# Weight loads ordered behind the newest transposes of queries and keys, and output stores behind the newest transpose of probabilities, in a two-layer attention trunk

## The chip, the cores and the metric

The kernel runs on one core of a Trainium2 chip. The metric is the device time of one execution in microseconds (us). TensorE (PE) multiplies matrices, VectorE (DVE), ScalarE (ACT) and GpSimd (POOL) work on tiles element by element, and SyncE (SP) issues every DMA of this kernel, all on one queue.

## The reference

Two layers on a sequence of 1024 tokens with width 1024. Layer 0 mixes tokens by dilated sliding-window attention (mixer A, three groups, merged by their softmax denominators), layer 1 by grouped-query attention with a window of 128 and learned sinks (mixer B). Shortened:

```python
def reference(x, p, ...):
    for i in range(DEPTH):                      # DEPTH = 2
        h = mixer_a(...) if i % 3 == 0 else mixer_b(...)
        x = layer_norm(ALPHA * x + h, ln_g[i], ln_b[i])
        gate = sigmoid(x @ ple_w_gate[i])
        x = x + gate * (p[i] @ ple_w_proj[i])

def mixer_a(x, w_in, w_out, cos, sin):
    h = x @ w_in
    for gi, (window, dil) in enumerate(A_GROUPS):    # (128,1), (512,4), (2048,16)
        q, k, v = ...                                # 16 heads of 64, q and k rotated
        o, lse = banded_attention(strided(q), strided(k), strided(v), window // dil)
    o = sum over groups of softmax(lse) * o
    return (o * silu(z)) @ w_out
```

`banded_attention` takes softmax(q k / 8) over a causal band and multiplies by v.

## The kernel before

**Linear products.** Each weight matrix is cut into blocks of 512 columns (33 blocks, numbered here in the order of their use; layer A has blocks 0 to 19 of its input matrix, then 20 and 21 of its output matrix). `Block.load` (line 97) brings a block in four DMAs of 512 KB (`wraw`, line 102). `maxima` (line 108, DVE) finds its largest value, `split` (lines 131 and 132, ACT and DVE) writes it as two float16 parts. `weight_steps` strings this together: block i+2 is loaded as soon as block i has been split, since there are two buffers for `wraw`. `lin` (lines 270 to 272) makes one 128x512 tile of a product from 24 matmuls, in about 5.2 us.

**Attention.** In layer A a run of three blocks is values, queries and keys, queries and keys. After each tile of queries and keys `rope_out` rotates it on DVE and POOL (lines 345 to 359) and transposes it by a DMA, `qk<-hl` (line 360; `bq` and `bk` in layer B). A "unit" is 128 queries of four heads. `scores` multiplies queries and keys (line 383), takes the mask and the row maximum on DVE (line 387), the exponentials on ACT (line 393), splits the probabilities into two float16 parts (lines 397 and 399) and transposes them by a DMA, `pT<-phl` (line 402, the P transpose). `pv` multiplies the transposed probabilities by the values (lines 414 to 416). `outp` evicts the result to `st` and stores it to DRAM, `scr<-st` (line 703). There are 96 units in layer A and 32 in layer B, numbered here from 0 in the order in which they are scored. A unit's `pv` is issued two units after its scores in layer A, three in layer B, so that softmax and transpose have time meanwhile. Layer A's outputs are read back (`gt<-scr`, line 745), merged over the three groups (`merge`) and stored (`oa<-gt`, line 767). In layer B the stores are `ob<-mu` (line 860), and the gate's rows are `za<-zu` and `zb<-zu` (line 725).

**What sets the order.** The kernel is written as one stream of operations; a scheduler, which works with estimated durations, puts each engine's instructions into an order. On the chip an engine takes its own in that order and waits where one's inputs are not there. SP too is such an engine: a DMA whose buffer is not free holds up all DMAs behind it.

Of the kernel before, what the change touches and what calls it, by code (L numbers as in the profile page):

```python
# [2 lines left out]

# [1 line left out]

# [83 lines left out]
class Block:  # L89
# [5 lines left out]

    def load(self):
        k = self.k
        self.n = NK * self.cols
        self.raw = k.raw.tile([P, NK * 512], F32, tag="wraw", name="wraw")
        q = self.n // 4  # L100
        for c in range(4):
            k.nc.sync.dma_start(self.raw[:, c * q:(c + 1) * q], self.src[:, c * q:(c + 1) * q])
# [36 lines left out]
class Trunk:  # L139
    def __init__(self, ctx, tc, a):  # L140
        self.ctx, self.tc, self.nc, self.a = ctx, tc, tc.nc, a
        nc = self.nc
        ec = ctx.enter_context
        self.const = ec(tc.tile_pool(name="const", bufs=1))
        self.small = ec(tc.tile_pool(name="small", bufs=2))
        self.raw = ec(tc.tile_pool(name="raw", bufs=2))
        self.wp = ec(tc.tile_pool(name="wp", bufs=2))
        self.ps_lin = ec(tc.tile_pool(name="ps_lin", bufs=3, space=PSUM))
        self.ps_s = ec(tc.tile_pool(name="ps_s", bufs=4, space=PSUM))
        self.ps_o = ec(tc.tile_pool(name="ps_o", bufs=1, space=PSUM))  # L150
        self.dram = ec(tc.tile_pool(name="dram", bufs=1, space=DRAM))
        self.o_ps = self.ps_o.tile([P, 2, 4, HD], F32, tag="o", name="o")
        self.o_i = 0
        self.uid = 0
        self.bufs = 2
        self.pw = self.wg = None
        self.due = []
        self.merges, self.merging = [], []
        self.merge_wait, self.merge_every = 0, 1
        self.units = []  # L160
        self.upt = 1.0
        self.pipe = [None, None]
        self.credit = 0.0
        self.ends = []
        self.work_done = 0.0
        self.tile_w = 1.0
        self.step_credit = 0.0

        tab = self.const.tile([P, N_CONST], F32, name="tab")
        self.tab = tab  # L170
        b = 0
        self.mask_a = tab[:, b:b + 2 * P]
        self.mask_b = tab[:, b + 2 * P:b + 4 * P]
        self.mask_2 = tab[:, b + 4 * P:b + 5 * P]
        self.ident = tab[:, b + 5 * P:b + 6 * P]
        self.ones = self.const.tile([P, P], BF16, name="ones")
        nc.gpsimd.memset(self.ones, 1.0)
        self.ones32 = self.const.tile([P, 1], F32, name="ones32")
        nc.gpsimd.memset(self.ones32, 1.0)
        self.mhalf = self.const.tile([P, 1], F32, name="mhalf")  # L180
        nc.gpsimd.memset(self.mhalf, -0.5)
        self.sinks = self.const.tile([P, 16], F32, name="sinks")
# [152 lines left out]
    def rope_out(self, ps, nq, nk, n, dst):  # L335

        nc, w = self.nc, self.work
        nh = nq + nk  # L340
        t1 = w.tile([P, 512], F32, tag="t1", name="t1")
        t2 = w.tile([P, 512], F32, tag="t2", name="t2")
        pv = ps.rearrange("p (h c) -> p h c", c=32)
        cos = self.cos[:, n, :].unsqueeze(1).to_broadcast([P, 2 * nh, 32])
        nc.vector.tensor_mul(t1[:, :nh * HD].rearrange("p (h c) -> p h c", c=32), pv, cos)  # L345
        pb = ps.rearrange("p (h b c) -> p h b c", b=2, c=32)[:, :, ::-1, :]
        sin = self.sin[:, n].unsqueeze(1).to_broadcast([P, nh, 2, 32])
        nc.vector.tensor_mul(t2[:, :nh * HD].rearrange("p (h b c) -> p h b c", b=2, c=32), pb, sin)  # L348
        nc.gpsimd.tensor_add(t1[:, :nh * HD], t1[:, :nh * HD], t2[:, :nh * HD])  # L349
        nb = nh + nk  # L350
        hl = w.tile([P, 12, P], F16, tag="hl", name="hl", bufs=3)
        rv = t1[:, :nh * HD].rearrange("p (h c) -> p h c", c=HD)

        def parts():
            nc.scalar.activation(hl[:, :nh, 0:HD], rv, AF.Copy)  # L355
            nc.gpsimd.tensor_sub(hl[:, :nh, HD:P], rv, hl[:, :nh, 0:HD])  # L356
            if nk:
                src, to = (hl[:, a:b, :].rearrange("p h (w c) -> p h w c", w=2) for a, b in ((nq, nh), (nh, nb)))
                nc.vector.tensor_copy(to, src[:, :, ::-1, :])  # L359
            nc.sync.dma_start(dst, hl[:, :nb, :].rearrange("p b c -> p (b c)"), transpose=True)  # L360

        self.ends.append(parts)

# [6 lines left out]
    def scores(self, qa, kas, mask, cs, ncs, sums, nbias, floor, pool_lo):  # L370
# [28 lines left out]
        eng.tensor_sub(hl[:, 1], sm[:, :, :nk], hl[:, 0])  # L399
        pt = at.tile([P, 2, 4, 2, P], F16, tag="pT", name="pT", bufs=len(self.pipe) + 1)  # L400
        ptf = pt.rearrange("p a h b c -> p (a h b) c")[:, :8 * nb, :]
        nc.sync.dma_start(ptf, pf[:, :8 * nk], transpose=True)
        return ptf.rearrange("p (a h b) c -> p a h b c", a=2, h=4)

    def pv(self, pt, va, vla):
# [278 lines left out]
    def unit_a(self, q, g, n, qk, vh, vl, cs, ncs, cv, scr):  # L684
        nc, at = self.nc, self.att
        tiles = [n] if g == 2 or (n % 2 == 0 if g == 1 else n == 0) else [n - 1, n]
        mask = self.mask_2 if g == 2 else self.mask_a[:, (2 - len(tiles)) * P:]

        def stats():
            st = at.tile([P, 4 * HD + 8], F32, tag="st", name="st", bufs=len(self.pipe) + 2)  # L690
            return st, st[:, 4 * HD:4 * HD + 4], st[:, 4 * HD + 4:]

        def outp(o, st):
            nc.scalar.activation(st[:, 0:4 * HD], o.rearrange("p h c -> p (h c)"), AF.Copy, scale=cv)
            d = scr[q // 2][g][:, q % 2, :]
            if g == 1:
                b = 512 * (n % 2) + n // 2
                d = d[b:b + 509:4]
            elif g == 2:
                d = d[n:n + 1017:8]  # L700
            else:
                d = d[n * P:(n + 1) * P]
            nc.sync.dma_start(d, st)
            if g == 0 and q % 2:
                self.merges.append(self.merge(n, q // 2, scr[q // 2]))

        kas = [lambda h, sw, t=qk[i]: t[:, 4 + 4 * sw + h, :] for i in tiles]
        self.later(UNIT_LAG, lambda: self.unit(lambda h: qk[n][:, h, :], kas, mask, cs, ncs,
                                          lambda h, kb: vh[:, tiles[kb], h, :], lambda h, kb: vl[:, tiles[kb], h, :],
                                          stats, outp, n % 4 != 0))  # L710
# [16 lines left out]
    def z_block(self, invx, stat):  # L727

        self.z_stat = stat
        self.upt = 2.0  # L730
        for half in range(2):
            self.w_z = self.next_block()
            self.cz = self.prod(invx, self.w_z.inv, 0.5, "cz")
            for n in range(Z_AHEAD if half else NT):
                self.z_tile(self.work, n, half)
                self.progress()
            if half == 0:
                self.w_z.released = True
# [405 lines left out]
```

## Time and profile before

| what | value |
|---|---|
| median of 3 runs | 1685.56 us (1683.73 to 1686.35) |
| the profiled execution | 1685.33 us |
| its span, first to last instruction | 1683.5 us |
| PE busy | 1595.0 us, 95% of the span |
| mean granted TensorE clock | 0.984 |

The table says that PE works nearly all the time, so a microsecond is won or lost where PE stands idle or runs at its lower clock. A PE that is "busy" is not at its peak: matmuls overlap in the record. What counts is the interval from one start to the next.

### The profile page before, as it was taken

The page shows a single profiled execution, that of the slowest core. Times are in us where ns is not written, and L with a number is a line of the kernel's source. Part 1 is how long each engine was busy: PE and PEld are TensorE (multiplying, and loading weights), DVE is VectorE, ACT ScalarE, POOL GpSimd, SP SyncE. Part 2 cuts the span into 40 slices and gives each one's busy share as a digit, 9 for nine tenths or more (in the row PEclk, how much of TensorE's full clock was granted, in tenths as well). Part 3 has the DMA queues.
Part 4 walks back from the last instruction along what each step waited for, and adds up shares of the span by engine and source line. Part 5 has one row for each costly group of instructions (what it writes and reads, how often), then busy time and mean ns, then how long its engine had stood idle before and what let it go on. Part 6 is the DMA issues. An engine that isn't in the chain of part 4 may idle for free. (4 is left out here: it accounts for less than half of the span.)

```text
span 1683.5 us, 29019 instructions
## 1 busy us (share of the span) xinstructions
PE 1595.0 (95%) x10579; PEld 881.5 (52%) x10579; DVE 1130.6 (67%) x2721; ACT 871.7 (52%) x1946; POOL 677.5 (40%) x481
## 2 busy tenths in 40 slices
PE   9898999999999889999999988898999998999999
PEld 3455566654555445766545544344455555544444
DVE  6767556665667776566656696887447898778631
ACT  4525564564755355655647662633232888853321
POOL 0215423532554565234325654443323552225441
PEclk9999999999999999999999999899999999999999
DMA  9617855773678668557647986989965798987963
GB/s 361 242 60 160 171 145 123 174 159 108 140 160 219 190 137 176 151 132 163 155 114 157 193 224 208 316 242 276 233 179 133 139 207 176 182 292 219 248 209 113
DMA packets 543791, 311.02 MB, mean 185 GB/s; under 512 B 473120, under 2 KB 494240, under 8 KB 543392
## 3 DMA queue, kind: packets, MB, share of 16 engines
q1 hardware_dynamic: 543648, 309.16, 74.1%
q8 instruction: 83, 1.36, 0.3%
q14 instruction: 60, 0.49, 0.1%
HBM read 137.78 MB, written 54.92 MB: 114 GB/s over the span
## 5 line engine op out<-in xcount | busy, mean ns | idle before, releaser
L270 PE MATMUL lin<-whl,xhl 128*128 128x512 f16 x1280 | 491.2, 384 | 0.0
L271 PE MATMUL lin<-whl,xhl 128*128 128x512 f16 x1280 | 490.3, 383 | 0.0
L272 PE MATMUL lin<-whl,xhl 128*128 128x512 f16 x1280 | 489.9, 383 | 0.0
L349 POOL TENSOR_TENSOR t<-t,t 128x512 f32<-128x512 f32 (+1 forms) x120 | 152.4, 1270 | 265.2 <-DVE t L348 233.0
L399 POOL TENSOR_TENSOR phl<-sm,phl 128x1024 f16<-128x1024 f32 (+1 forms) x88 | 156.9, 1783 | 245.4 <-ACT phl L397 217.8
L108 DVE TENSOR_REDUCE wpm<-wraw 128x1 f32<-128x1024 f32 (+1 forms) x132 | 157.1, 1198 | 92.6 <-DMA wraw<-in_wa_dram 48.2
L272 PEld LDWEIGHTS <-xhl 128*128 128x128 f16 x1280 | 149.5, 117 | 128.0 <-issue 5.3
L270 PEld LDWEIGHTS <-xhl 128*128 128x128 f16 x1280 | 149.5, 117 | 120.1 <-issue 5.4
L271 PEld LDWEIGHTS <-xhl 128*128 128x128 f16 x1280 | 150.4, 117 | 118.1 <-issue 5.3
L393 ACT ACTIVATE sm<-sm,st,cs 128x128 f32<-128x128 f32 (+1 forms) x384 | 203.6, 532 | 3.8 <-ACT mw L752 0.3
L356 POOL TENSOR_TENSOR hl<-t,hl 128x512 f16<-128x512 f32 (+1 forms) x120 | 145.4, 1212 | 124.6 <-ACT hl L355 124.6
L387 DVE CUSTOM_DVE_ANT_0 sm<-s,tab 128x256 f32<-128x256 f32 (+1 forms) x512 | 156.9, 359 | 33.6 <-PE s L383 31.9
L355 ACT ACTIVATE hl<-t 128x512 f16<-128x512 f32 (+1 forms) x120 | 72.3, 603 | 190.6 <-POOL t L349 181.5
L132 DVE SCALAR_TENSOR_TENSOR whl<-wraw,s,whl 128x1024 f16<-128x1024 f32 (+1 forms) x116 | 161.4, 1445 | 3.1 <-ACT whl L131 3.0
L131 ACT ACTIVATE whl<-wraw,s 128x1024 f16<-128x1024 f32 (+1 forms) x116 | 121.9, 1123 | 26.6 <-PE lin L272 10.2
L270 PE MATMUL lin<-whl,x2T 128*128 128x512 f16 (+1 forms) x320 | 115.5, 361 | 0.0
L271 PE MATMUL lin<-whl,x2T 128*128 128x512 f16 (+1 forms) x320 | 115.2, 360 | 0.0
L272 PE MATMUL lin<-whl,x2T 128*128 128x512 f16 (+1 forms) x320 | 115.2, 360 | 0.0
L397 ACT ACTIVATE phl<-sm 128x1024 f16<-128x1024 f32 (+1 forms) x128 | 110.7, 865 | 3.6 <-DMA pT<-phl 1.6
L345 DVE TENSOR_TENSOR t<-lin,rope 128x512 f32<-128x512 f32 (+1 forms) x120 | 78.9, 658 | 47.2 <-PE lin L272 46.9
L359 DVE COPY hl<-hl 128x512 f16<-128x512 f16 (+1 forms) x104 | 55.7, 535 | 74.7 <-POOL hl L356 74.6
L414 PEld LDWEIGHTS <-pT 128*128 128x128 f16 x800 | 72.8, 99 | 46.4 <-DMA pT<-phl 44.0
(190 smaller groups left out, 2913.7 us busy)
## 6 DMA issues: line engine op xcount, KB each, us to landing
wraw<-in_wa_dram SPq DMA_DIRECT2D x56, 512.0 KB, 5.1
scr<-st SPq DMA_DIRECT2D x96, 132.0 KB, 2.4
gt<-scr SPq DMA_DIRECT2D x48, 264.0 KB, 3.5
wraw<-in_wav_dram SPq DMA_DIRECT2D x24, 512.0 KB, 5.6
prh<-pro SPq DMA_DIRECT2D x32, 256.0 KB, 4.4
wraw<-in_wg_dram SPq DMA_DIRECT2D x16, 512.0 KB, 7.7
wraw<-in_wb_dram SPq DMA_DIRECT2D x16, 512.0 KB, 6.7
xg<-y SPq DMA_DIRECT2D x16, 512.0 KB, 3.8
```

What stands on the lines that cost most here:

```text
L108: k.nc.vector.tensor_reduce(pm[:, c:c + 1], self.raw[:, c * q:(c + 1) * q], axis=AX.X, op=ALU.max, apply_absolute_value=True)
L131: nc.scalar.activation(hl[:, 0, sl], self.raw[:, sl], AF.Copy, scale=self.s)
L132: nc.vector.scalar_tensor_tensor(hl[:, 1, sl], self.raw[:, sl], self.s, hl[:, 0, sl], op0=ALU.mult, op1=ALU.subtract)
L270: mm(ps, xh(kt), wh, start=(kt == 0), stop=False)
L271: mm(ps, xh(kt), wl, start=False, stop=False)
L272: mm(ps, xl(kt), wh, start=False, stop=(kt == NK - 1))
L349: nc.gpsimd.tensor_add(t1[:, :nh * HD], t1[:, :nh * HD], t2[:, :nh * HD])
L356: nc.gpsimd.tensor_sub(hl[:, :nh, HD:P], rv, hl[:, :nh, 0:HD])
L387: nc.vector.tensor_tensor_reduce(sm[:, h, :nk], ps[:, i, :nk], mask, 1.0, -3e38, ALU.add, ALU.max, mx[:, h:h + 1])
L393: nc.scalar.activation(sm[:, h, :nk], sm[:, h, :nk], AF.Exp, bias=nbias[:, h:h + 1], scale=cs, accum_out=sums[:, h:h + 1])
L397: nc.scalar.activation(hl[:, 0], sm[:, :, :nk], AF.Copy)
L399: eng.tensor_sub(hl[:, 1], sm[:, :, :nk], hl[:, 0])
```

## The change

Two ties are added, both by `issue_after(ins)`, which lays an ordering edge (no wait on a semaphore) from an instruction to those that the block issues on the same engine, here SP. First, the four DMAs of a weight load stand behind the transpose of queries and keys that was written last (`self.moved`) when `load` is called; `z_block` clears this mark, so that loads called from there on are free until layer B's first transpose. Second, the store of a unit in layer A stands behind the P transpose that was written last (`self.p_moved`), which is that of a unit scored later. Nothing is computed differently, and no instruction is added or removed on any engine.

```diff
     def load(self):
+        k = self.k
+        with k.tc.issue_after(k.moved.ins) if k.moved else nullcontext():
+            self.transfers()
+
+    def transfers(self):
         k = self.k
         self.n = NK * self.cols
         self.raw = k.raw.tile([P, NK * 512], F32, tag="wraw", name="wraw")
...
         self.o_i = 0
         self.uid = 0
+        self.moved = self.p_moved = None
...
-            nc.sync.dma_start(dst, hl[:, :nb, :].rearrange("p b c -> p (b c)"), transpose=True)
+            self.moved = nc.sync.dma_start(dst, hl[:, :nb, :].rearrange("p b c -> p (b c)"), transpose=True)
...
-        nc.sync.dma_start(ptf, pf[:, :8 * nk], transpose=True)
+        self.p_moved = nc.sync.dma_start(ptf, pf[:, :8 * nk], transpose=True)
...
-            nc.sync.dma_start(d, st)
+            with self.tc.issue_after(self.p_moved.ins):
+                nc.sync.dma_start(d, st)
...
     def z_block(self, invx, stat):
 
         self.z_stat = stat
+        self.moved = None
         self.upt = 2.0
```

Since the scheduler starts anew from these edges, the order changes in other places too. (The changed file has eight more lines, so line 402 is line 408 there, 360 is 366, 102 is 107, 703 is 710, 414 is 420, 270 to 272 are 276 to 278 and 383 is 389.)

SP's queue at the load of block 11 (`wraw_5139`), while layer A's tiles 39 to 44 of queries and keys are made (`qk_` and `pT_` with their numbers are the transposes; `scr0` is a store). Before:

```order
L703 DMA scr0_0_617<-st_4511 128x264
L102 DMA wraw_5139<-in_wa_dram 128x1024
L360 DMA_TRANSPOSE qk_4724<-hl_4730 128x12x128
L402 DMA_TRANSPOSE pT_4764<-phl_4761 128x16x128
L703 DMA scr0_0_617<-st_4613 128x264
L360 DMA_TRANSPOSE qk_4828<-hl_4834 128x12x128
L102 DMA wraw_5139<-in_wa_dram 128x1024 x3
L402 DMA_TRANSPOSE pT_4885<-phl_4882 128x16x128
```

Now:

```order
L366 DMA_TRANSPOSE qk_4724<-hl_4730 128x12x128
L408 DMA_TRANSPOSE pT_4764<-phl_4761 128x16x128
L710 DMA scr0_0_617<-st_4511 128x264
L366 DMA_TRANSPOSE qk_4828<-hl_4834 128x12x128
L408 DMA_TRANSPOSE pT_4885<-phl_4882 128x16x128
L710 DMA scr0_0_617<-st_4613 128x264
...
L366 DMA_TRANSPOSE qk_5067<-hl_5073 128x12x128
L107 DMA wraw_5139<-in_wa_dram 128x1024 x4
L408 DMA_TRANSPOSE pT_5107<-phl_5104 128x16x128
```

The four loads move from around the 40th and 41st transpose of queries and keys to behind the 44th, and stand in one piece. Before, three of them were directly ahead of `pT_4885` (unit 37); now all four are directly ahead of `pT_5107` (unit 39). The store of `st_4511` moves past one P transpose. Twelve of layer A's load groups (blocks 4, 5, 7, 8, 10, 11, 13, 14, 16, 17, 19, 20) move like this by four or five transposes of queries and keys; those of blocks 6, 9, 12, 15 and 18, at the end of a run, stay within one transpose of where they were. On DVE the maxima of the twelve blocks move with the loads, and the splits stay where they were. After the move a P transpose stands directly behind such loads, with no other transpose between, for nine units: 3, 7, 17, 33, 39, 49, 55, 65 and 81. For blocks 8, 17 and 20 a transpose of queries and keys stands between. In layer B the loads of blocks 27 to 29 move likewise by four or five transposes.

PE's order at the first product of unit 42 (`pT_5452`), at the end of layer A's first half. Before:

```order
L383 LDWEIGHTS qk_5172
L383 MATMUL s_5656<-qk_5172 128x128
L414 LDWEIGHTS pT_5452
L414 MATMUL o_78<-vh_648,pT_5452 128x64
```

Now:

```order
L277 MATMUL lin_5731<-whl_4839,xhl_106 128x512
L278 LDWEIGHTS xhl_106
L278 MATMUL lin_5731<-whl_4839,xhl_106 128x512
L420 LDWEIGHTS pT_5452
L420 MATMUL o_78<-vh_648,pT_5452 128x64
```

The product now stands 42 rows later, behind 21 further matmuls of 128x512. That of unit 49 moves later by ten such matmuls. Other units of layer A move little or not at all.

PE's order in layer B at the first product of unit 109 (`pT_15002`; `bq` and `bk` are queries and keys). Before:

```order
L383 LDWEIGHTS bq_14778
L383 MATMUL s_15415<-bk_13446,bq_14778 128x128
L414 LDWEIGHTS pT_15002
L414 MATMUL o_78<-bvh_13454,pT_15002 128x64
```

Now:

```order
L389 LDWEIGHTS bq_14676
L389 MATMUL s_15332<-bk_13446,bq_14676 128x128
L420 LDWEIGHTS pT_15002
L420 MATMUL o_78<-bvh_13454,pT_15002 128x64
```

It now stands among the scores of an earlier tile, 52 rows, that is 26 matmuls, earlier. The products of units 105 to 127 all move earlier in this way, by roughly the same, while their scores stay within a few matmuls of where they were.

## Rows read from the trace of the kernel before

**Rows 1.** The page, part 1: busy us, share of span, instructions.

```profile
PE 1595.0 (95%) x10579; PEld 881.5 (52%) x10579; DVE 1130.6 (67%) x2721; ACT 871.7 (52%) x1946; POOL 677.5 (40%) x481
```

**Rows 2.** PE's waits, whole span: for what, us in total, times, longest.

```profile
PE o L414 <- DMA pT<-phl: 32.4, 21, 3.8
...
PE s L383 <- DMA qk<-hl: 6.3, 4, 3.6
```

**Rows 3.** SP's waits, whole span.

```profile
SPq L102 <- DVE whl L132: 85.4, 20, 22.2
```

**Rows 4.** SP's timeline, 462 to 477 us: start, duration, line, DMA, count.

```profile
465.34 1.66 SPq L102 DMA_DIRECT2D wraw<-in_wa_dram  x3
467.11 5.89 SPq L402 DMA_TRANSPOSE pT<-phl  x1
```

**Rows 5.** PE's timeline at four P products; idle before them in brackets.

```profile
475.99 0.20 PE L414 MATMUL o<-vh,pT 128*128 128x64 f16 x1 [1.71 <-DMA pT<-phl]
...
642.48 0.20 PE L414 MATMUL o<-vh,pT 128*128 128x64 f16 x1 [1.05 <-DMA pT<-phl]
...
786.52 0.20 PE L414 MATMUL o<-vh,pT 128*128 128x64 f16 x1 [1.26 <-DMA pT<-phl]
...
935.67 0.20 PE L414 MATMUL o<-vh,pT 128*128 128x64 f16 x1 [1.53 <-DMA pT<-phl]
```

**Rows 6.** DMA to landing of P transposes: 80 to 510 us, then 777 to 780.

```profile
DMA to landing us min/median/max: 2.7/3.7/8.8
DMA to landing us min/median/max: 7.6/7.6/7.6
```

**Rows 7.** PE's timeline at the first products of units 42 and 49.

```profile
522.43 0.23 PE L414 MATMUL o<-vh,pT 128*128 128x64 f16 x1 [3.48 <-DMA pT<-phl]
...
616.38 0.20 PE L414 MATMUL o<-vh,pT 128*128 128x64 f16 x1 [2.86 <-DMA pT<-phl]
```

**Rows 8.** PE's timeline, 599 to 601 us: four matmuls of a tile, two shown.

```profile
599.69 0.38 PE L272 MATMUL lin<-whl,xhl 128*128 128x512 f16 x1
...
600.34 0.38 PE L272 MATMUL lin<-whl,xhl 128*128 128x512 f16 x1
```

**Rows 9.** Two stretches: busy PE, PEld, DVE, ACT, POOL; granted clock; DMA; GB/s.

```profile
515.00:522.00 7.00, 3.95 (x31) 2.34 (x28) 4.63 (x17) 4.75 (x13) 1.49 (x1) 0.97 1.18 255
522.00:529.00 7.00, 6.57 (x38) 3.22 (x39) 4.56 (x7) 0.47 (x1) 4.41 (x4) 0.54 0.95 304
```

**Rows 10.** PE's timeline at three waits near loads: scores, scores, P product.

```profile
141.05 0.62 PE L383 MATMUL s<-qk 128*128 128x128 f16 x8 [1.06 <-DMA qk<-hl]
...
1296.83 0.69 PE L383 MATMUL s<-bk,bq 128*128 128x128 f16 x5 [2.68 <-DMA bq<-hl]
...
1358.84 0.20 PE L414 MATMUL o<-bvh,pT 128*128 128x64 f16 x1 [2.97 <-DVE mx L387]
```

**Rows 11.** SP's timeline at the P transposes of units 39, 42 and 55.

```profile
489.30 2.06 SPq L402 DMA_TRANSPOSE pT<-phl  x1
...
516.18 4.18 SPq L402 DMA_TRANSPOSE pT<-phl  x1
...
659.99 1.58 SPq L402 DMA_TRANSPOSE pT<-phl  x1
```

**Rows 12.** PE's timeline at the products of units 39 and 55.

```profile
493.57 0.20 PE L414 MATMUL o<-vh,pT 128*128 128x64 f16 x1 [0.42 <-DMA pT<-phl]
...
665.93 0.19 PE L414 MATMUL o<-vh,pT 128*128 128x64 f16 x1
```

**Rows 13.** SP's timeline, 1376 to 1396 us: P transposes of units 109 and 110.

```profile
1375.49 5.51 SPq L402 DMA_TRANSPOSE pT<-phl  x2
```

**Rows 14.** DMA to landing of P transposes, 1376.5 to 1382 us.

```profile
DMA to landing us min/median/max: 4.8/5.1/5.4
```

**Rows 15.** PE's timeline at the first product of unit 109.

```profile
1385.25 0.19 PE L414 MATMUL o<-bvh,pT 128*128 128x64 f16 x1
```

**Rows 16.** SP's timeline behind the load of block 29, 1336 to 1360 us.

```profile
1350.01 8.91 SPq L402 DMA_TRANSPOSE pT<-phl  x2
```

More of the change, by code (lines that the diff above doesn't have):

```diff
@@ L1 @@
 import math
-from contextlib import ExitStack
+from contextlib import ExitStack, nullcontext
 import numpy as np
```

## Prediction

> **What bounds the kernel now.** I read the page first: PE is busy for 1595.0 us, 95% of the span [rows 1], so the time is PE's own work plus what PE waits. The table of PE's waits comes next. The reader is to see in it that the largest one is for P transposes, 32.4 us in 21 waits, and that scores wait 6.3 us for transposed queries and keys [rows 2]. These two are what the change can reach. The third view is SP's waits: 20 weight loads stood at the head of the queue for 85.4 us, the longest 22.2 us, until a split had freed their buffer [rows 3]. One would conclude that loads block transposes at the head of the queue. SP's timeline shows another thing: three loads are issued in 1.66 us, the P transpose behind them at 467.11 [rows 4], and PE starts its product only at 475.99, after 1.71 us of idleness ended by that transpose [rows 5]. That is 8.9 us after the issue, where the median from issue to landing is 3.7 us and the most 8.8 us [rows 6]. So what makes a transpose late is less the wait for a buffer than the data of the loads ahead of it. A change that puts the loads elsewhere in the queue moves this lateness to another transpose, and the question is how much slack that one has.
>
> **The change part by part.** Nothing is added or removed on an engine, so all cost and gain lies in waits. The sum is made against the profiled execution, 1685.33 us, of which 1683.5 us are span; it is 0.2 us from the median of the three runs.
>
> First, loads leave their old places. Behind the old places PE waits 1.71, 1.05, 1.26 and 1.53 us at four P products [rows 5], for the loads of blocks 11, 14, 17 and 20. Together 5.6 us, and I take all of it as gained.
>
> Second, two P products come later in PE's order. Unit 42 waits 3.48 us [rows 7]; it moves behind 21 more matmuls of 128x512. Three matmuls take 600.34 - 599.69 = 0.65 us [rows 8], one 0.217 us, so 21 take 4.5 us. Its product would be wanted at 522.43 - 3.48 + 4.5 = 523.5 us. But its transpose now has four loads ahead, so that it is issued later than the 516.2 us of today [rows 11] by up to four times 1.66 / 3 = 0.55 us [rows 4], of which I take 1.7 us, and, at 7.6 us to land as behind another load [rows 6], lands at about 525.5. So 2.0 us of wait stay and 1.5 us are gained. Unit 49 moves by ten matmuls, 2.2 us, and its transpose no longer stands behind one of queries and keys; its 2.86 us [rows 7] go. A wait also has a second price: in the 7 us up to 522 PE is busy for 3.95 us at a clock of 0.97, and in the 7 us after that the granted clock is 0.54 [rows 9], the lower of the two levels, 1.2 GHz, for nearly all of it. That costs up to 7 x (1 - 0.54) = 3.2 us for the wait of unit 42, and by the same row half as much for unit 49's shorter one. Since 2.0 us of wait stay, I take half of the 4.8 us: 2.4 us. Together 1.5 + 2.9 + 2.4 = 6.8 us.
>
> Third, scores near loads: 1.06 us at 141 us in layer A and 2.68 us at 1297 us in layer B [rows 10] wait for transposes of queries that stand behind loads; after the change no load is near them. That is 3.7 us.
>
> Fourth, layer B's load of block 29: the two P transposes behind it need 8.91 us to be issued [rows 16], and PE waits 2.97 us at 1358.84 [rows 10]. The view names a DVE instruction there, but that row of SP ends within 0.1 us of the product's start, so I read it as the transpose. The loads leave this place: 3.0 us.
>
> Fifth, the new places, a cost. Nine P transposes now stand directly behind loads. Two examples: unit 39's is issued at 489.30 [rows 11] and its product starts at 493.57, after a wait of 0.42 us [rows 12]. Four loads ahead put the issue 1.7 us later, and with 7.6 us to land [rows 6] the product would start at 498.6, 5.0 us later. Unit 55's is issued at 659.99 [rows 11], its product starts at 665.93 with no wait [rows 12]; with 7.6 us it would be 667.6, 1.7 us later. Bounds from these: nothing, if the loads are issued early enough to be through before P is ready (they follow a transpose of queries, which often comes some us sooner), and nine times 5.0 = 45 us if all are as unit 39. The nearest rows are the four of [rows 5], where the same thing now happens and costs 1.4 us on average, and some such loads now cost PE nothing. I take half of the waits' mean and a little, 0.8 us, nine times: 7.0 us.
>
> Sixth, layer B's P products move earlier, a cost. Unit 109's transpose is issued at 1375.49 [rows 13], lands at most 5.4 us later [rows 14], at 1380.9, and its product starts at 1385.25 [rows 15]: 4.3 us of slack. It moves ahead of 26 matmuls, at most 26 x 0.217 = 5.6 us. So up to 1.3 us are missing here. All units from 105 on are moved by about as much, and a wait that is paid once delays the later products too, so I bound it by nothing and 5.6 us and take 3.0 us.
>
> At nothing I cost three things. The loads come up to five tiles later, but the splits stay where they were on DVE, so no product waits for weights; PE's largest waits now are others [rows 2], and if that cover went, a load's 7.6 us would be paid once per block. The maxima move along with their loads. The stores move behind one P transpose: PE does not wait for a store, and only the merges read them; if the merges at a half's end came late by one unit, about 8 us, the rows of the output product would be late at the end of layer A.
>
> Sum: -5.6 - 6.8 - 3.7 - 3.0 + 7.0 + 3.0 = -9.1 us, so 1676.2 us.
>
> On the fifth part the Trainium skill speaks against the change. Its page "DMA: Bandwidth & Descriptors", section "Queues, rings and completion order", says that each DMA engine consumes the descriptors of a queue in ring order; a transpose behind four loads then waits for their data wherever they stand. The trace agrees where a transpose follows loads (8.9 us against 3.7). By that rule alone the fifth part would be paid at all nine places, which is the rival below.
>
> **The rivals.** Slower: the data of the loads is paid in full at the nine new places. For this speaks that loads and transpose are now adjacent, four loads instead of three; against it that in the half from unit 48 on several transposes behind loads cost nothing. At the mean of the two examples, (5.0 + 1.7) / 2 = 3.4 us, nine cost 30 us, and the sum is -19.1 + 30 + 3.0 = +14 us: 1699 us. It decides from (19.1 - 3.0 + 3.4) / 9 = 2.2 us a place on.
>
> No difference: the waits only change places, since the same bytes go through the same queue. At 1.8 us a place the gain of 19.1 us is met by 16 + 3: 1685 us.
>
> A larger gain: loads follow a transpose of queries at once, when P is not ready yet, so the fifth part costs nothing, the full 4.8 us of clock come back, and layer B's slack suffices. For this speaks that a load at the queue's head no longer waits for its buffer. -19.1 - 2.4 = -21.5 us: 1664 us.
>
> **How the numbers follow.** A measurement of this kernel tells some 0.2%, 3.4 us, from no change. My forecast, 1670 to 1682 us, has 0.48, the larger gain 0.12, no difference 0.18, slower 0.22. So faster 0.60, same 0.18, slower 0.22. The predicted time is 1676.2 us. The range from 1663 to 1692 leaves out most of the slower case and little else.
>
> **What would show it.** In the changed kernel's profile PE's waits for P transposes fall from 32.4 to about 20 us and those for queries to below 4. At the nine units PE's timeline shows waits of 0 to 2 us, and the landing behind loads stays near 7 to 9 us. SP's wait for splits at loads nearly vanishes. The wait of unit 42 is below 2.5 us. In layer B short waits for P transposes appear. The prediction is wrong if PE's waits at the nine places average over 2 us, if layer B's waits grow by more than 6 us, or if a wait of several us turns up for something that I costed at nothing: weights, merges or maxima on DVE.

## The result, and the profile after

The change made the kernel slower. The median went from 1685.95 us (four runs, 1683.73 to 1687.28) to 1709.71 us (four runs, 1708.26 to 1716.11): a ratio of 1.0148 over the runs (1.0141 by the medians), 95% interval 1.0132 to 1.0164. The forecast was 1676.2 us, its range ended at 1692. The profiled execution of the changed kernel took 1716.11 us (span 1714.2 us), so it is the slowest of the four and lies 6.4 us above the median; that of before took 1685.33 us.

What answers to [rows 1], from the page of the changed kernel (busy us, share, instructions):

```profile
PE 1602.1 (93%) x10579; PEld 884.4 (52%) x10579; DVE 1127.5 (66%) x2721; ACT 871.8 (51%) x1946; POOL 682.2 (40%) x481
```

And to [rows 2, 3], the waits over the whole span of the changed kernel (us in total, times, longest):

```profile
PE o L420 <- DMA pT<-phl: 52.6, 34, 4.4
...
PE s L389 <- DMA qk<-hl: 8.9, 4, 5.3
...
SPq L107 <- DVE whl L137: 34.0, 5, 22.1
```

The loads' waits at the head of the queue did fall, from 85.4 to 34.0 us, and it brought nothing: PE's waits for P transposes rose from 32.4 to 52.6 us, where I had expected 20, and those for queries and keys from 6.3 to 8.9 us, where I had expected less than 4.

Where was the time lost? Two marks cut both kernels alike: the last matmul of layer A's last P product (it starts at 1011.92 us before and at 1033.91 us after) and the first product of layer 0's gate (1171.18 and 1199.12 us). Three stretches of the kernel before, layer A from 125 us on, the merge with the output product, and the rest (length, busy PE, PEld, DVE, ACT, POOL, granted clock, DMA share, GB/s):

```profile
125.00:1012.00 887.00, 849.33 (x6155) 505.14 (x6153) 588.65 (x1526) 507.26 (x1282) 411.84 (x297) 0.99 0.70 160
1012.00:1171.00 159.00, 139.48 (x629) 61.67 (x626) 124.92 (x260) 65.55 (x83) 71.15 (x43) 0.96 0.89 258
1171.00:1683.00 512.00, 490.62 (x3345) 258.84 (x3343) 330.72 (x784) 247.79 (x515) 179.27 (x128) 0.99 0.81 196
```

The same three in the changed kernel:

```profile
125.00:1034.00 909.00, 856.46 (x6156) 508.90 (x6155) 578.96 (x1526) 506.59 (x1282) 415.24 (x295) 0.98 0.68 156
1034.00:1199.00 165.00, 142.08 (x627) 62.12 (x624) 124.74 (x257) 63.81 (x82) 70.55 (x45) 0.94 0.87 249
1199.00:1714.00 515.00, 487.76 (x3345) 257.09 (x3343) 337.44 (x787) 250.18 (x518) 181.12 (x129) 1.00 0.78 195
```

The reader is to see that 22 of 31 us are lost in layer A, with the same number of matmuls. Of these 22, PE idles 909 - 856.46 = 52.5 us in place of 887 - 849.33 = 37.7 us, 14.9 us more; the other 7.1 us are busy time, at a granted clock of 0.98 after 0.99. The merge and the output product lose 6 us, layer B and the end 3 us.

PE's waits at the new places, in the timeline of the changed kernel: units 3, 7, 33, 39, 42, 49, 55 and 81, then unit 74 (idle time before it in brackets):

```profile
164.14 0.20 PE L420 MATMUL o<-vh,pT 128*128 128x64 f16 x1 [1.60 <-DMA pT<-phl]
...
202.43 0.23 PE L420 MATMUL o<-vh,pT 128*128 128x64 f16 x1 [4.38 <-DMA pT<-phl]
...
448.53 0.20 PE L420 MATMUL o<-vh,pT 128*128 128x64 f16 x1 [1.93 <-DMA pT<-phl]
...
500.53 0.20 PE L420 MATMUL o<-vh,pT 128*128 128x64 f16 x1 [1.22 <-DMA pT<-phl]
...
534.28 0.23 PE L420 MATMUL o<-vh,pT 128*128 128x64 f16 x1 [3.84 <-DMA pT<-phl]
...
626.16 0.20 PE L420 MATMUL o<-vh,pT 128*128 128x64 f16 x1 [1.86 <-DMA pT<-phl]
...
675.98 0.23 PE L420 MATMUL o<-vh,pT 128*128 128x64 f16 x1 [4.28 <-DMA pT<-phl]
...
921.76 0.20 PE L420 MATMUL o<-vh,pT 128*128 128x64 f16 x1 [0.84 <-DMA pT<-phl]
...
849.96 0.22 PE L420 MATMUL o<-vh,pT 128*128 128x64 f16 x1 [3.09 <-DMA pT<-phl]
```

At the nine units that stand directly behind loads the waits are 1.60, 4.38, 1.93, 1.22, 1.86, 4.28, 0.84 and twice nothing (units 17 and 65, where two of the four loads stand behind the transpose): 16.1 us, 1.8 us a place. Three of these units waited in the kernel before too: unit 3 for 3.28 us, unit 39 for 0.42 [rows 12], unit 49 for 2.86 [rows 7], together 6.6 us. Unit 42 waits 3.84 us, after 3.48 before [rows 7]. What such a place looks like on SP, for units 7 and 55 (start, duration, line, DMA, count):

```profile
189.65 2.36 SPq L107 DMA_DIRECT2D wraw<-in_wa_dram  x4
192.36 7.11 SPq L408 DMA_TRANSPOSE pT<-phl  x1
...
663.66 2.32 SPq L107 DMA_DIRECT2D wraw<-in_wa_dram  x4
666.60 6.44 SPq L408 DMA_TRANSPOSE pT<-phl  x1
```

Unit 55's transpose took 1.58 us to issue before [rows 11] and takes 6.44 us now; its product came without a wait [rows 12] and comes 4.28 us late now. It lands 9.3 us after its issue:

```profile
DMA to landing us min/median/max: 9.3/9.3/9.3
```

PE wanted it at 675.98 - 4.28 = 671.70 us, 5.1 us after the issue at 666.60, so at the 3.7 us that are the median in layer A it would have been in time. That holds for all seven places that wait: their transposes land 8.4 to 10.3 us after the issue, and PE wanted them 5.1 to 8.8 us after it. Unit 74, which stands at none of the nine places, waits too; one load stands directly ahead of its transpose, which lands after 5.3 us where others of its size take 2.7:

```profile
843.67 0.88 SPq L107 DMA_DIRECT2D wraw<-in_wa_dram  x1
844.65 1.24 SPq L408 DMA_TRANSPOSE pT<-phl  x1
```

DVE's timeline shows another thing, at the maxima of block 17:

```profile
824.23 2.46 DVE L113 TENSOR_REDUCE wpm<-wraw 128x1 f32<-128x1024 f32 x2 [3.06 <-DMA wraw<-in_wa_dram]
826.60 0.28 DVE L393 CUSTOM_DVE_ANT_0 sm<-s,tab 128x128 f32<-128x128 f32 x1
```

DVE stands 3.06 us at a maximum whose load has not landed, with two maxima to do then, and behind them in its queue is a unit's row maximum (`sm<-s`), whose scores have been ready since 823.58. (The Trainium skill, page "TensorE: Matmul & The Clock Gate", section "Architectural detail: the array is 16× 32×32, not 1× 128×128", says that DVE takes its queue strictly in order; these two rows agree.) This unit, number 73, starts its softmax 3.0 us late, but had that to spare: its product comes without a wait. Nowhere in layer A of this profile does PE wait more than 0.75 us for a unit whose row maximum DVE held up in this way, so these rows show a possible way, and its price they do not show. The groups of instructions give the sum, 106.8 us of idle DVE ahead of the weights' maxima in the changed kernel (132 of them; busy, mean ns, idle and what ended it), where the kernel before has 92.6:

```profile
L113 DVE TENSOR_REDUCE wpm<-wraw 128x1 f32<-128x1024 f32 (+1 forms) x132 | 157.1, 1198 | 106.8 <-DMA wraw<-in_wa_dram 54.7 <-DMA wraw<-in_wav_dram 30.5 <-DMA wraw<-in_bo_dram 6.8
```

### The profile page after: what moved, and what is told of

Read it like the earlier page. It is cut to its first block, busy times and chain, and to the rows that moved or that the text cites. A ratio compares the mean times of both kernels' runs of the same rounds, so it can differ in the third digit from the quotient of the medians.

```text
span 1714.2 us, 28951 instructions
## 1 busy us (share of the span) xinstructions
PE 1602.1 (93%) x10579; PEld 884.4 (52%) x10579; DVE 1127.5 (66%) x2721; ACT 871.8 (51%) x1946; POOL 682.2 (40%) x481
## 5 line engine op out<-in xcount | busy, mean ns | idle before, releaser
L113 DVE TENSOR_REDUCE wpm<-wraw 128x1 f32<-128x1024 f32 (+1 forms) x132 | 157.1, 1198 | 106.8 <-DMA wraw<-in_wa_dram 54.7
L137 DVE SCALAR_TENSOR_TENSOR whl<-wraw,s,whl 128x1024 f16<-128x1024 f32 (+1 forms) x116 | 165.1, 1469 | 4.8 <-ACT whl L136 4.7
L365 DVE COPY hl<-hl 128x512 f16<-128x512 f16 (+1 forms) x104 | 52.5, 504 | 109.2 <-POOL hl L362 109.0
```

Of the source, the lines that this page charges most:

```text
L113: k.nc.vector.tensor_reduce(pm[:, c:c + 1], self.raw[:, c * q:(c + 1) * q], axis=AX.X, op=ALU.max, apply_absolute_value=True)
L137: nc.vector.scalar_tensor_tensor(hl[:, 1, sl], self.raw[:, sl], self.s, hl[:, 0, sl], op0=ALU.mult, op1=ALU.subtract)
```

## The experiments

For each run the table has the ratio to the kernel before with its interval, the start of the last matmul of layer A's P products ("A end"), that of the gate's first product ("gate"), PE's waits for P transposes and DVE's idle time ahead of weights' maxima, all in us. "Behind qk" means that loads are tied as the change ties them, "behind P" that they are tied behind the newest P transpose.

| run | loads; maxima | ratio (95%) | A end | gate | P waits | DVE idle |
|---|---|---|---|---|---|---|
| before | free; near | 1 | 1011.92 | 1171.18 | 32.4 | 92.6 |
| after | behind qk, stores tied; near | 1.0148 (1.0132 to 1.0164) | 1033.91 | 1199.12 | 52.6 | 106.8 |
| e1_loads_only | behind qk; near | 1.0151 (1.0130 to 1.0173) | 1028.53 | 1197.95 | 49.5 | 111.7 |
| e2_stores_only | free, stores tied; near | 1.0108 (1.0089 to 1.0127) | 1020.56 | 1187.65 | 38.2 | 105.0 |
| e3_loads_b | layer B only; near | 1.0009 (0.9997 to 1.0020) | 1011.14 | 1172.49 | 31.7 | 93.4 |
| e4_behind_p | behind P; near | 1.0120 (1.0090 to 1.0150) | 1014.33 | 1183.92 | 30.5 | 81.5 |
| e9_behind_p_a | behind P in A; near | 1.0031 (1.0014 to 1.0047) | 1013.36 | 1177.51 | 37.3 | 81.7 |
| e5_half_after | as after, half data; near | 1.0107 (1.0073 to 1.0140) | 1012.69 | 1182.65 | 33.1 | 68.1 |
| e6_half_before | free, half data; near | 0.9915 (0.9890 to 0.9941) | 998.45 | 1160.63 | 17.7 | 53.3 |
| e7_lag3_after | as after, lag 3; near | 1.0181 (1.0158 to 1.0204) | 1025.37 | 1194.94 | 19.0 | 113.9 |
| e8_lag3_before | free, lag 3; near | 1.0031 (1.0010 to 1.0052) | 1006.03 | 1176.76 | 11.6 | 113.7 |
| e12_small_after | as after; short | 1.0097 (1.0065 to 1.0129) | 1035.67 | 1185.99 | 49.6 | 157.3 |
| e13_small_before | free; short | 0.9895 (0.9871 to 0.9919) | 1003.87 | 1151.71 | 28.8 | 141.5 |
| e11_maxima_late | free; late | 0.9959 (0.9943 to 0.9976) | 1004.55 | 1169.92 | 30.1 | 41.0 |
| e16_after_later | as after; late | 1.0135 (1.0104 to 1.0166) | 1018.53 | 1192.85 | 34.6 | 56.6 |
| e20_after_later_19 | as after; late | 1.0139 (1.0121 to 1.0157) | 1013.80 | 1192.18 | 37.5 | 59.3 |
| e17_behind_p_later | behind P in A; late | 0.9959 (0.9945 to 0.9974) | 999.83 | 1168.34 | 18.9 | 52.3 |
| e21_behind_p_later_all | behind P in A; all late | 0.9954 (0.9938 to 0.9971) | 1001.82 | 1166.84 | 18.4 | 30.9 |
| e18_before_all_late | free; all late | 0.9943 (0.9922 to 0.9964) | 996.97 | 1160.54 | 24.8 | 22.5 |
| e19_half_after_later | as after, half data; late | 0.9970 (0.9955 to 0.9985) | 997.45 | 1167.77 | 14.9 | 38.5 |

"Near" maxima are where the scheduler puts them; "late" ones are tied behind later tiles, one or two tiles later in e16, e17, e19, e20 and e21 than in e11 and e18. Ratios come from several runs, the other columns from one profile each, which lies as much as 8.5 us below (e12) or 6.4 us above (the changed kernel) the median of its runs. Before and e3_loads_b, alike up to layer B, differ by 0.8 us at the first mark and 1.3 us at the second; from one order to another the PE work ahead of the first mark differs by up to 3 us, for e16_after_later by 4.

**The ties one by one.** e1_loads_only drops the stores' tie:

```diff
-            with self.tc.issue_after(self.p_moved.ins):
+            with nullcontext():
```

> The tie of the loads alone; the stores are free as before. Theory (the loads' new places in layer A cost, directly ahead of P transposes): nearly all of the loss is here, 1.011 to 1.016 times the kernel before, about 1708 us. Rival (stores that come one unit later hold up the queue for transposes and merges): 1.000 to 1.004, about 1688 us. Rival (the scheduler's other new places, which any of the ties sets off): between, near 1.007.

e2_stores_only drops the loads' tie:

```diff
-        with k.tc.issue_after(k.moved.ins) if k.moved else nullcontext():
+        with nullcontext():
```

> The tie of the stores alone; the loads are free as before. Theory of the loads' new places: 0.997 to 1.003, about 1685 us, since PE waits for no store. Rival of the stores: 1.008 to 1.015, about 1705 us. Rival of the other new places: about 1.007.

e3_loads_b drops the stores' tie and keeps that of loads in layer B alone:

```diff
-        with k.tc.issue_after(k.moved.ins) if k.moved else nullcontext():
+        with k.tc.issue_after(k.moved.ins) if k.moved and len(k.pipe) == 3 else nullcontext():
```

> The tie of the loads in layer B alone (blocks from the first transpose of keys in layer B on); layer A's loads and all stores are free. Theory of layer A's new places: 0.999 to 1.004, at most 6 us slower. Rival (layer B's P products, which come earlier in PE's order, and the loads there cost most of the loss): 1.008 or more.

Measured: 1.0151, 1.0108 and 1.0009. The loads' tie alone makes the whole loss, so the theory held there; the stores' tie alone costs 18 us too, which the theory did not allow and the rival of the stores had forecast, and the two don't add. Layer B is not where it is lost.

**Another place for the loads.** e4_behind_p:

```diff
-        with k.tc.issue_after(k.moved.ins) if k.moved else nullcontext():
+        with k.tc.issue_after(k.p_moved.ins) if k.moved else nullcontext():
```

> Loads tied behind the newest P transpose in place of the newest transpose of queries and keys, stores free. Of the twelve groups of loads that the change put into the middle of a run, all but a few now stand directly ahead of a transpose of queries and keys. Theory (what costs is that a P transpose, with a few us of slack, stands directly behind the loads): the loss falls to less than half, 0.998 to 1.005, about 1688 us. Rival (the loads' data holds up whatever comes behind them, and one transpose is as short of time as the other): as the change, 1.010 to 1.016. A third outcome, below 0.997, would make it a better kernel than both.

By time it looks like the rival, 1.0120. By the marks it does not: layer A ends at 1014.33, 14.2 us ahead of e1_loads_only, and P waits are back at 30.5 us; the loss lies behind that mark, where 12.7 us in all have gathered at the gate. e9_behind_p_a takes the tie away there (`k.moved and len(k.pipe) == 2 and k.blocks.index(self) < 18` as its condition):

> Loads tied behind the newest P transpose as in e4, but only in layer A and only for blocks below 18; stores, layer A's last blocks and layer B free. If the loss of e4 came from the merge and layer B alone, as its trace shows (layer A ended level with the kernel before): 0.997 to 1.002. If the order in layer A itself brings the later loss along: 1.005 or more.

1.0031, just above its expectation. So where loads stand matters; that left open why.

**Less data, more slack.** e5_half_after and e6_half_before load half the columns and read them twice:

```diff
-            k.nc.sync.dma_start(self.raw[:, c * q:(c + 1) * q], self.src[:, c * q:(c + 1) * q])
+            k.nc.sync.dma_start(self.raw[:, c * q:c * q + q // 2], self.src[:, c * q:c * q + q // 2])
```

> The changed kernel, each load fetching only half of its columns; maxima and splits read that half twice, so that they take as long as ever, and the weights are not the reference's. The loads stand where the change put them, directly ahead of the P transposes of the same nine units. Theory (the loads' data in the queue ahead of a P transpose is the price, and it is over the few us that its product has to spare): with half the data the lateness mostly fits, and the kernel is within 8 us of the same cut made to the kernel before (e6). Rival (the other reordering on PE and DVE, which the bytes don't touch): still 20 us or more above e6.

> The control to e5: the kernel before with the same half loads (weights are not the reference's). By the theory it gains too, since some P transposes of the kernel before stand behind loads: 0.990 to 0.997. If the waits for P transposes have nothing to do with loads' data, 1.000.

e7_lag3_after and e8_lag3_before give each P product one more unit of lag:

```diff
-        self.set_lag(2)
+        self.set_lag(3)
...
-                        qk.append(at.tile([P, 12, P], F16, tag="qk", name="qk", bufs=8))
+                        qk.append(at.tile([P, 12, P], F16, tag="qk", name="qk", bufs=6))
```

> The changed kernel with one more unit between scores and P product in layer A (three, as in layer B; the buffers of transposed queries and keys are cut from eight to six to make room). Loads and transposes stand side by side as in the changed kernel, but a P product has some 8 us more to spare. Theory: layer A's loss of about 20 us goes, that in the merge and in layer B stays: within 10 us of its control e8. Rival (loss by the issue order as such): 20 us or more above e8.

> The control to e7: the kernel before with one more unit of lag in layer A and six buffers of transposed queries and keys. Theory: its own waits for P transposes in layer A, some 20 us, mostly go too, 0.988 to 0.998; six buffers in place of eight may cost some of it.

Both pairs went against the theory: 31 us between e5 and e6, 26 us between e7 and e8, in layer A 14.2 and 19.3 us. By themselves e6 came out as expected (0.9915), and e8 missed (1.0031): more lag did not help the kernel before. With half the data a P transpose lands after 6.6 us at most in place of 10.3 (from the row of the P transposes, 80 to 1010 us), and still layer A keeps most of the loss. With more lag P waits fall to 19.0 us, and others take their place (waits of PE in e7_lag3_after):

```profile
PE o L420 <- DMA pT<-phl: 19.0, 12, 3.7
PE lin L276 <- DVE wpm L113: 18.3, 1, 18.3
PE o L420 <- ACT st L700: 17.2, 10, 3.4
```

The 18.3 us are one wait, of the output product's first matmul; for the 17.2 us e8 has 13.9. What e8's layer A has none of are three waits of PE, 8.4 us together, that end with a row maximum on DVE. DVE's and PE's timelines of e7_lag3_after at one of them:

```profile
664.83 2.52 DVE L113 TENSOR_REDUCE wpm<-wraw 128x1 f32<-128x1024 f32 x2 [4.72 <-DMA wraw<-in_wa_dram]
...
673.92 0.41 DVE L393 CUSTOM_DVE_ANT_0 sm<-s,tab 128x256 f32<-128x256 f32 x1
...
674.74 0.40 PE L389 MATMUL s<-qk 128*128 128x128 f16 x4 [2.97 <-DVE mx L393]
```

DVE stands 4.72 us at a maximum, works on from there with one more wait of 0.67 us, again for a load, and comes late to the row maximum that PE's next scores wait for. So something makes units late before their transposes, and here one can see it.

**DVE's maxima.** Second theory: the 4.8 us of maxima a block now lie among the row maxima. e11_maxima_late keeps the kernel before and moves the maxima alone (`BEHIND` gives for each block the tile of queries and keys; `ropes` are DVE's rotations):

```diff
         for c in range(4):
-            k.nc.vector.tensor_reduce(pm[:, c:c + 1], self.raw[:, c * q:(c + 1) * q], axis=AX.X, op=ALU.max,
-                                      apply_absolute_value=True)
+            with k.tc.issue_after(k.ropes[min(n, len(k.ropes)) - 1].ins) if n else nullcontext():
+                k.nc.vector.tensor_reduce(pm[:, c:c + 1], self.raw[:, c * q:(c + 1) * q], axis=AX.X, op=ALU.max,
+                                          apply_absolute_value=True)
```

> The kernel before with its loads and stores where they were; only the maxima of the twelve blocks are tied on DVE to the place where the change has them, four or five tiles later, among the units' row maxima. New theory (DVE's late maxima, 4.9 us a block, delay the softmax of the units beside them, so that P is ready too late): most of layer A's loss is here, 1.006 to 1.011, 1695 to 1703 us. First theory (the loads' data ahead of P transposes): 0.998 to 1.002.

e12_small_after and e13_small_before shorten the maxima from 1.2 to 0.28 us:

```diff
-            k.nc.vector.tensor_reduce(pm[:, c:c + 1], self.raw[:, c * q:(c + 1) * q], axis=AX.X, op=ALU.max,
+            k.nc.vector.tensor_reduce(pm[:, c:c + 1], self.raw[:, c * q:c * q + q // 8], axis=AX.X, op=ALU.max,
```

> The changed kernel with maxima that read an eighth of their columns (their scales are then not the reference's), in the same places, so that a block's maxima are short on DVE; loads and all else as in the changed kernel. New theory (DVE): at most 14 us above its control e13. First theory (loads' data): still 20 us or more above e13.

> The control to e12: the kernel before with the same short maxima. DVE gets 4 us a block back, of which little is on the path: 0.992 to 0.999 by either theory.

The second theory fell: late maxima gained 7 us, against both expectations, and short ones left 36 us between e12 and e13 (e13 gained 1.05%, a little more than expected). But the column of DVE's idle time pointed at a reason. In e12 the maxima are short and DVE's wait for their data grows, to 157.3 us; in e11 it falls to 41.0 us. Third theory: DVE's standing at the maxima until a load has landed, ahead of the row maxima, makes P ready late; and behind it the loads' data makes the P transpose land late. By this theory either is enough to make a unit late. The idle time is no price by itself: in e13 it rises too, from 92.6 to 141.5 us, and layer A ends 8.1 us sooner, so there the maxima's own length does cost.

**Both ways closed.** e16_after_later is the changed kernel with the maxima one or two tiles later still:

```diff
+BEHIND = {4: 8, 5: 14, 7: 23, 8: 31, 10: 39, 11: 47, 13: 55, 14: 63, 16: 71, 17: 79, 19: 87, 20: 95}
```

> The changed kernel with its loads and stores where they are; the maxima of the twelve blocks are tied on DVE one or two tiles later still, so that their data should be there when DVE comes to them. Third theory (DVE waits for the loads' data ahead of the units' row maxima, which makes P ready late; and P transposes behind loads take the rest): DVE's waits at maxima fall from 107 to some 45 us, about half of layer A's 21 us comes back, 1.004 to 1.009. First theory alone (loads' data ahead of P transposes): unchanged, 1.012 to 1.017. A loss by the order as such: unchanged too.

e19_half_after_later joins that to the half loads of e5:

> The changed kernel with half loads (as e5, 1.011; weights are not the reference's) and the late maxima of e16: neither much data ahead of a P transpose, nor DVE waiting for it. Third theory: nothing of layer A's loss is left, and the whole comes within 10 us of e6, the kernel before with half loads (0.9915), so 0.990 to 0.998. If 1.005 or more, a further cause is at work.

e17_behind_p_later has e16's late maxima and e9's loads:

> Loads in layer A tied behind the newest P transpose (as e9, which was 1.003), stores free, and the maxima late as in e16. Third theory: both ways in which a load reaches a unit are closed, so it gains on e9 by some 8 to 15 us and beats the kernel before, 0.992 to 0.998. If DVE's waits at maxima don't matter: as e9, 1.001 to 1.005.

e18_before_all_late ties the values' blocks as well, to the kernel before:

```diff
+UNITS = {6: 15, 9: 31, 12: 47, 15: 63, 18: 79}
...
+        n = BEHIND.get(i) or UNITS.get(i, 0)
+        at = k.ropes if i in BEHIND else k.rows
```

> The kernel before with the late maxima of e11 (which was 0.996), and those of the values' blocks 6, 9, 12, 15 and 18 tied behind the row maxima of the last units of their run as well. Third theory: a few us better than e11, 0.991 to 0.996. If e11's gain had another cause: as e11 or worse, 0.996 to 1.000.

e17, e18 and e19 came out as the third theory says; e19 has no control, since the kernel before with half the loads and late maxima was not run. e16 did not in time, 1.0135, though layer A ended 15.4 us sooner than in the changed kernel: one wait of 19.9 us at the output product took it. I laid that to block 20's late maxima; e20_after_later_19 leaves out `20: 95`:

> As e16, the changed kernel with late maxima, but block 20's are left free, since its late weights cost 20 us in the output product there. Third theory: layer A within 5 us of the kernel before, the merge and layer B as in the changed kernel, some 9 us: 1.003 to 1.009. If the loss in layer A only moves elsewhere: 1.011 or more.

That guess was wrong: 1.0139. Layer A ends within 2 us of the kernel before (1013.80), DVE no longer waits at block 17's maxima,

```profile
813.59 4.59 DVE L115 TENSOR_REDUCE wpm<-wraw 128x1 f32<-128x1024 f32 x4
```

and yet the output product's first matmul stands 18.95 us:

```profile
1092.32 0.59 PE L282 MATMUL lin<-whl,ogT 128*128 128x512 f16 x1 [18.95 <-issue]
```

The view names nothing for it. I read what it waits for as a chain that begins at the last store of a merge (`oa<-gt`), since the next stage's buffers take the place of layer A's. ACT's timeline shows the start of it, at the split of the second half of the output weights, in e20_after_later_19:

```profile
1066.44 2.19 ACT L138 ACTIVATE wo<-wraw,s 128x1024 f16<-128x1024 f32 x2 [5.97 <-DMA oa<-gt]
```

and in the kernel before, 13.9 us earlier:

```profile
1052.58 3.23 ACT L131 ACTIVATE wo<-wraw,s 128x1024 f16<-128x1024 f32 x3 [7.56 <-DMA oa<-gt]
```

SP's timeline shows its end in e20, the transpose of the first rows, which the matmul above reads:

```profile
1083.62 6.45 SPq L888 DMA_TRANSPOSE ogT<-rhl  x1
```

From the issue of the last merge's store to the output product's first matmul it is 27.6 us before (1050.2 to 1077.83), 28.1 us in the changed kernel (1075.2 to 1103.34) and 28.1 us in e20 (1064.21 to 1092.32); in all kernels with full loads, full maxima and a lag of two it is 27.6 to 28.2 us. So layer A has a second end, that of its merges: that store is issued 38.3 us behind the first mark before, 41.3 us in the changed kernel and 50.4 us in e20. Time won in layer A is given back there when the merges end no sooner.

e21_behind_p_later_all puts all remedies on loads behind P (`6: 18, 9: 34, 12: 50, 15: 66, 18: 82` added, block 20 free):

> The version that the experiments point to: loads of layer A behind the newest P transpose, stores free, the maxima of blocks 4 to 19, the values' included, two tiles or so behind their loads, block 20 free. e17 had layer A 16 us below the kernel before and lost 11 us of it in the output product. Third theory: 0.987 to 0.994; if the loss there has another cause than block 20's maxima, as e17, 0.995 to 0.998.

0.9954, no better than e17. Of the kernels with full loads and full maxima e18_before_all_late has the lowest ratio, 0.9943 (1676.86 us), with loads and stores free; its interval overlaps those of e11, e17 and e21. Its page shows 1589.9 us of busy PE and its group of maxima the remedy:

```profile
L116 DVE TENSOR_REDUCE wpm<-wraw 128x1 f32<-128x1024 f32 (+1 forms) x132 | 152.8, 1194 | 22.5 <-DMA wraw<-in_wb_dram 7.6 <-DMA wraw<-in_wa_dram 4.8 <-DMA wraw<-in_bo_dram 3.9
```

## Why the prediction was wrong

The sign was wrong. The rival that I called slower came nearest, with 1699 us, but not by its own way: it needed 3.4 us a place, and 1.8 were measured. By the steps:

- **Fifth, the new places: the step that failed first.** I took 0.8 us nine times, 7.0 us; the nine waits are 16.1 us. My reason, that the loads would often be through before P is ready, held at two places; at the other seven the transposes landed 8.4 to 10.3 us after the issue, where I had reckoned with 7.6. (For unit 55 I left out the later issue that I gave unit 39: I had 1.7 us late, and it waits 4.28; unit 39, where I had 5.0, waits 1.22.) Of the 12.5 us that PE waits more for P transposes in layer A (43.4 after 30.9), 16.1 - 6.6 = 9.5 are here. That the place of the loads sets layer A's end is seen with stores free in e1 and e4 (1028.53 behind qk, 1014.33 behind P, 14.2 us), and with less of DVE's waits in e20 and e17: 1013.80 with loads behind qk, 999.83 behind P, at nearly the same idle DVE (59.3 and 52.3 us), and P waits fall from 37.5 to 18.9 us; the first of these two has the stores' tie as well. With this term alone put right the sum gives 1685 us, no difference, so it is not the whole miss.
- **"The maxima move along with their loads", costed at nothing.** This is what I did not see at all. DVE's wait for a load's data stood in the profile before, 92.6 us, as the idle time of an engine that is not the bottleneck, and I did not ask what is queued behind it. Late maxima bring layer A's end 20.1 us forward in the changed kernel (1033.91 to 1013.80) and 7.4 us in the kernel before (1011.92 to 1004.55); so of the 22.0 us that the change lost there, about 20.1 - 7.4 = 12.7 us would hang on it. The size is not settled: with e16 in place of e20 it is 15.4 - 7.4 = 8.0 us, and with e18 as the control, where the values' maxima are late too, 20.1 - 15.0 = 5.1 us. By the same reckoning half the data takes away 21.2 - 13.5 = 7.8 us. All these come from single profiles. In the whole time little of it came back: with late maxima the changed kernel still takes 1.0135 and 1.0139.
- **First, old places.** 5.6 us were to be gained. Unit 37's wait is gone, but unit 68 waits 2.16 us at 798.55 with no load near, and at the four units together 3.4 us are still waited.
- **Second, units 42 and 49.** 6.8 us were to be gained. Their waits are 3.84 and 1.86 us after 3.48 and 2.86 [rows 7]; unit 42's later place was eaten by four loads ahead, for which I had sized the landing at 7.6 us; it took 9.3.
- **Third, fourth and sixth, mostly layer B.** The waits of 1.06, 2.68 and 2.97 us [rows 10] went, as forecast, but others for queries and keys in layer A grew, to 8.9 us after 6.3; the earlier P products cost more than 3.0 us, PE's waits for P transposes in layer B and behind it being 9.2 us after 1.4. Together I had -2.7 us in layer B, and e3_loads_b gives +0.09%, nothing that can be told.
- **The stores, at nothing.** Alone they cost 1.08%. Layer A ends 8.6 us later in e2_stores_only and the gate starts another 7.8 us later. DVE's idle time at maxima is 105.0 us there, though the maxima of blocks 4 to 19 stand behind the same row maxima as before; why it grows is open. My bound of 8 us for late merges is near the 7.8 us, and between the marks the change itself lost 6 us. Neither was tested by itself.
- **The clock.** I let half of 4.8 us come back; layer A's busy time grew by 7.1 us. In the 7 us behind unit 7's wait the granted clock is 0.55, nearly all at 1.2 GHz:

```profile
202.00:209.00 7.00, 6.58 (x39) 3.36 (x40) 5.16 (x24) 4.91 (x12) 2.32 (x3) 0.55 1.04 172
```

Of the three signs that I named for a wrong prediction, the first came close (1.8 us a place, where I had drawn the line at 2), the second as good as came (+7.8 us of P waits in layer B, with others gone), and the third came for what I had costed at nothing, the merges and the maxima on DVE, though as a longer stage and as idle time of DVE, not as a wait of PE that names them.

What stays open is how much of layer A's loss hangs on DVE's maxima, and what sets the merges' end: between the two marks the kernels need from 147.8 us (e13_small_before) to 178.4 us (e20_after_later_19), and no run took a part of it alone.

## What to carry to other kernels

Before an order is tied, look on every in-order engine for an instruction that waits for the moved transfer's data, and at what is queued behind it: here a weight's maximum that nobody needs soon stood ahead of row maxima, and putting it behind work that is ready gained 0.4 to 0.6% without any change to transfers. A wait removed at the head of a queue need not be a gain: here 51 us of them went, and PE then waited 9.5 us longer for the transposes at the loads' new places. And a stage has as many ends as it has chains: with late maxima the changed kernel's layer A ended 20 us sooner on PE, and the output product began only 11 us sooner (1103.34 to 1092.32).

## What the runs showed that I had not expected

At the seven new places that wait, a DMA transpose behind four loads of 512 KB takes 6.2 to 7.4 us to issue, where the median in layer A is 1.6 us, so the loads hold up the issuing queue too and not only the landing. An ordering edge on SP alone, with no instruction added, moved instructions on DVE and PE and cost 18 us (stores), where PE waits for none of the tied transfers itself. And two remedies that add up in one stage need not add up in the time: half the data brings layer A's end 21.2 us forward, late maxima (e16) 15.4, both 36.5 (1033.91 to 997.45), but each alone left 1.01 in time and both together 0.997, since between the marks half the data alone gave back 4.8 us, late maxima alone 9.1 and both together 5.1.
